# A hybrid decoder layer on one core: who issues the first loads, where the key memsets and the first products of zeros stand

## The chip, the cores and the metric

The kernel runs on one core of a Trainium2 chip. The metric is the device time of one execution in microseconds (us). A core has TensorE (PE: matrix products, with its weight loads in a queue of their own, PEld), VectorE (DVE), ScalarE (ACT), GpSimd (POOL) and SyncE (SP). SP, ScalarE and GpSimd can issue DMA transfers; sixteen DMA engines carry them.

## What is computed

One layer of a decoder for 1024 tokens of width 1024, ahead of which 16 learned meta tokens are put. Everything is in 32-bit floating point.

```python
h = jnp.concatenate([meta, x], axis=1)
u = rmsnorm(h, g_pre_mix[l])
z = u @ w_in[l]
q, k, v, xr, yr = jnp.split(z, split_at, axis=-1)
attn = sliding_window_attention_with_sinks(q, k, v, attn_sinks[l])   # window 128, 8 heads, 2 key heads
...
mix = jnp.concatenate([attn, rec], axis=-1) @ w_out[l]
h = h + rmsnorm(mix, g_post_mix[l])
u = rmsnorm(h, g_pre_ffn[l])
f = jnp.square(jax.nn.relu(u @ w_ff1[l])) @ w_ff2[l]
h = h + rmsnorm(f, g_post_ffn[l])
```

`rec` is a convolution of four steps, a gated linear recurrence over the 1040 tokens and a GeLU gate. The call to the attention is shortened; its heads are reshaped there.

## The kernel before

The kernel is one function, `hybrid_layer`, that lists instructions on tiles. A planner then orders each engine's instructions: it replays the list on a clock of its own, takes what is ready by its place in the list, assigns each tile a buffer of its group (a `slot` of a tag, or a `bank` of the accumulator memory) and adds the waits. Two helpers tie the order by hand where it matters: `behind(name, ins)` puts an instruction behind another one of the same engine, and `chained(e, ins)` (line 332) does so along a list, e = 0 for ScalarE and e = 1 for VectorE.

Every 32-bit operand of a product is split into a high and a low part, and a product is three: high by high, high by low, low by high. ScalarE makes the high part by a cast, VectorE the low part by a subtraction.

The start goes like this, with the lines of the profile. GpSimd makes the identity matrix for the transposes, clears two halves of the key tiles (L298), and makes small constants. SP issues the loads in the order of the list: the meta tokens (L142), two 128-row tiles of x (L147), the two norm weight vectors (L155, L156), the key and value columns of w_in and the first query columns (L384), then further tiles of x. ScalarE loads the table of its square root with a first root of one column (L82).

The norm of the 16 meta rows is `norm_rows`: a square with a sum on ScalarE (L254), the power -1/2 on GpSimd (L170, L176), a scale on VectorE (L260). The first two tiles of x go through `norm_first`. For the first tile the square is shared, half on ScalarE (L237) and half on VectorE (L242); for the second ScalarE squares the whole tile. Then come a root on ScalarE (L82), a reciprocal on VectorE (L199) and two scales of 128x512 (L248).

TensorE meanwhile multiplies zeros: twelve products of 512 columns and six of 256 (`load`, L309), which are never read. Then it transposes the normed rows in eight blocks of 128 columns (`transposed(0, xn)`, L358), each of three pieces (16 meta rows, two tiles of x), and the planner puts one product of zeros of 128 columns beside each block (L365). The banks of the blocks go round over the tags pt, o and s, two banks each. Of each block ScalarE takes the high half, scaled by the norm weight of the column (L117), and VectorE the low half (L118); the norm weights stand in `gcol`, one column per block, which TensorE turns (L160) and VectorE copies (L161). Among the first casts, ahead of blocks 0 and 1, stand two halves of the cast of the key weights (`key_casts`, L344).

With that the first 272 columns of the normed input, u, are there, and TensorE starts with their products for keys and values (`part`, L282): high weights by high u for the eight blocks, high weights by low u, then the same for the values, and the low weights. Queries follow, the next 256 tokens are transposed, and so on for four stages (`ALL`). The stages b = 1, 2, 3 norm their rows by `norm_rows` (in `normed`), two tiles each.

The tile `km` holds the first keys with zeros before them; GpSimd clears it (L412, L413) where the list stands behind the query weights. `vmt` holds the norm weights as rows first; GpSimd clears it later (L589) for other use.

From there on the kernel is products: attention with filling projections, the recurrence, the output projection, and the two large products of the feed-forward part, some of whose blocks are summed first.

Of the kernel before, what the change touches and what calls it, by code (L numbers as in the profile page):

```python
# [10 lines left out]
F32R = mybir.dt.float32r  # L11
AF = mybir.ActivationFunctionType
ALU = mybir.AluOpType
# [3 lines left out]
P = 128  # L17
# [3 lines left out]
NMETA = 16  # L21
# [16 lines left out]
def hybrid_layer(  # L38
# [6 lines left out]
    nc = tc.nc  # L45
# [12 lines left out]
    def slot(tag, shape, dt=F32):  # L58
        uid[0] += 1
        return slab.tile(shape, dt, tag=tag, name=f"{tag}{uid[0]}", bufs=bufs[tag])  # L60
# [4 lines left out]
    def bank(tag, shape=(P, 512)):  # L65
        uid[0] += 1
        return ps.tile(list(shape), F32, tag=tag, name=f"ps_{tag}{uid[0]}")

    def f32(ap):
        return ap.bitcast(F32)  # L70
# [8 lines left out]
    last_lut = [None]  # L79
# [58 lines left out]
    ident = const.tile([P, P], F32, name="ident")  # L138
    make_identity(nc, ident)

    meta_t = slot("d", [NMETA, D])
    nc.sync.dma_start(meta_t, meta_tokens)  # L142
    xt = []

    def load_x(i):
# [6 lines left out]

    vmt = const.tile([P, P], F32, name="vmt")
    g_r = vmt[0:16, :]
    nc.sync.dma_start(g_r[0:8, :], g_pre_mix.rearrange("o (k p) -> (o k) p", p=P))  # L155
    nc.sync.dma_start(g_r[8:16, :], g_pre_ffn.rearrange("o (k p) -> (o k) p", p=P))  # L156

    gcol = const.tile([P, 16], F32, name="gcol")
    pg = bank("o")
    nc.tensor.transpose(pg[:, :16], g_r, ident[:16, :16])  # L160
    nc.vector.tensor_copy(gcol, pg[:, :16])  # L161
    g_mix_col, g_ffn_col = gcol[:, 0:8], gcol[:, 8:16]

    half_pow = const.tile([P, 1], F32, name="half_pow")
# [19 lines left out]
    eps_col = const.tile([P, 1], F32, name="eps_col")  # L184
# [7 lines left out]

    load_root()

    def root_rstd(ssq, bias, n=P):
        sd = small.tile([P, 1], F32, name="sd", tag="sd")
        lut(sd[:n], ssq, AF.Sqrt, bias=bias)
        rs = small.tile([P, 1], F32, name="rs", tag="rs")
        nc.vector.reciprocal(rs[:n], sd[:n])  # L199
        return rs[:n]  # L200


# [29 lines left out]
    def norm_first(src, halves):  # L232

        xn = slot("d", [P, D])
        ss = [small.tile([P, 1], F32, name=f"hq{i}", tag=f"hq{i}") for i in range(2)]
        c = slice(0, 512 if halves else D)
        nc.scalar.activation(  # L237
            xn[:, c], src[:, c], AF.Square, scale=RMS_SC, accum_out=ss[0]
        )
        if halves:  # L240
            c = slice(512, D)
            nc.vector.tensor_tensor_reduce(  # L242
                out=xn[:, c], in0=src[:, c], in1=src[:, c], scale=RMS_SC * RMS_SC,
                scalar=EPS, op0=ALU.mult, op1=ALU.add, accum_out=ss[1],
            )
        rs = root_rstd(ss[0], ss[1] if halves else eps_col)
        for c in (slice(0, 512), slice(512, D)):
            nc.vector.tensor_scalar(xn[:, c], src[:, c], rs, None, op0=ALU.mult)  # L248
        return xn

    def norm_rows(src, n, link=False):
        xn = slot("d", [P, D])
# [46 lines left out]

    zeros = slot("ws", [P, 512], F32R)  # L300
    nc.vector.memset(f32(zeros), 0.0)

    flip = [0]

# [2 lines left out]
    def load(n, cols, after=None):  # L307
        for _ in range(n):
            ins = nc.tensor.matmul(  # L309
                idle[:, :cols], zeros[:, :P], zeros[:, :cols], start=True, stop=True,  # L310
                skip_group_check=True,
            ).ins
            if after:
                behind(after, ins)
        return ins.name

    load(12, 512)
    load(6, 256)

    def normed(b):  # L320
        if b == 0:
            return [
                (norm_rows(meta_t[:NMETA], NMETA), NMETA),
                (norm_first(xt[0], True), P), (norm_first(xt[1], False), P),
            ]
        rows = [(xt[2 * b], P), (xt[2 * b + 1], P)]
        return [(norm_rows(s[:m], m), m) for s, m in rows]


    last = [None, None]  # L330
# [20 lines left out]
    def transposed(b, xn, after=None):  # L351
        t0, n = ALL[b]
        for kc in range(KC):
            flip[0] += 1
            pt = bank(("pt", "o", "s")[flip[0] % 3])
            o = 0
            for s, m in xn:
                ins = nc.tensor.transpose(  # L358
                    pt[:, o : o + m], s[:m, kc * P : (kc + 1) * P], ident[:m, :m]
                )  # L360
                if after:
                    behind(after, ins.ins)
                o += m
            if b == 0:
                load(1, P, ins.ins.name)  # L365
            uh, ul = u[kc]
            if b == 0 and kc in (0, 1):
                key_casts.pop(0)()
            high = split_scaled(
                uh[:, t0 : t0 + n], ul[:, t0 : t0 + n], pt[:, :n],  # L370
                g_mix_col[:, kc : kc + 1],
            )
            if b == 0:
                chained(0, high[0])
                chained(1, high[1])
# [17 lines left out]
    xn = normed(0)  # L393
# [14 lines left out]
    low_w(wv, rv)  # L408
    wq = high_w(rq)
    low_w(wq, rq)  # L410
    km = slot("ws", [P, 4, 2 * P], F32R)
    nc.gpsimd.memset(f32(km[:, 0:2, 0 : P - NMETA]), 0.0)  # L412
    nc.gpsimd.memset(f32(km[:, 2:4, :]), 0.0)  # L413
    nsink = const.tile([P, 8], F32, name="nsink")
    nc.sync.dma_start(nsink, attn_sinks[0].partition_broadcast(P))
    prm_r = slot("d", [8, 512])
# [1211 lines left out]
```

## Time and profile before

| what | us |
|---|---|
| median of 3 runs | 948.82 (948.57 to 948.83) |
| the profiled execution | 949.06 |
| its span, first to last instruction | 947.4 |
| PE busy in the span | 936.9 |
| DVE, ACT, POOL busy | 664.3, 504.3, 133.9 |

The mean granted clock of TensorE in the span was 0.999. All rows of the profile come from the one profiled execution; starts are counted from the first instruction, and its own time stands beside the span because some time lies around it. A row of the timeline gives start, length, engine, line, operation, written tile <- read tiles and, in brackets, how long the engine idled ahead of it and what released it. A row of the chain of waits gives start and length of one piece of the chain that ended last. "SPq" is a DMA being issued by SP. "issue" is time in which the engine waited for nothing that the profile shows. Matmuls are pipelined, so rows of TensorE overlap.

### The profile page before, as it was taken

The numbers are of one execution on the slowest core, as the hardware profiler recorded it, in microseconds if no ns is written. First come the engines' busy times: TensorE is split into PE (matmuls) and PEld (weight loads), VectorE is DVE, ScalarE is ACT, GpSimd is POOL, SyncE is SP. The second block draws the span as 40 slices with busy tenths as digits, with TensorE's granted clock in tenths as the row PEclk, the third lists the DMA queues.
The fourth block names the chain that finished last, engine by engine and source line by source line (L and its number), as shares of the span: only waits on it lengthen the run. The fifth ranks groups of instructions, "written<-read, shape, count | busy, mean of one in ns | idle before, by whom it ended". The sixth has DMA issues, their size and how long they took to land.

```text
span 947.4 us, 12177 instructions
## 1 busy us (share of the span) xinstructions
PE 936.9 (99%) x4584; PEld 783.6 (83%) x4584; DVE 664.3 (70%) x848; ACT 504.3 (53%) x845; POOL 133.9 (14%) x205
## 2 busy tenths in 40 slices
PE   9999999999999999999999999999999999999996
PEld 8999999877788878888888888888888888888885
DVE  6667788889877987665544465476667676779883
ACT  8546765679434664443655575654533443445441
POOL 4104436430021200010000000001111000001201
PEclk9999999999999999999999999999999999999999
DMA  8220011104359659574422364334877756637924
GB/s 273 57 66 25 24 46 45 45 23 140 102 176 271 200 182 285 187 256 134 156 89 89 111 214 121 108 112 112 199 168 176 211 178 194 186 131 209 239 63 89
DMA packets 97366, 134.91 MB, mean 142 GB/s; under 512 B 22230, under 2 KB 61158, under 8 KB 97308
## 3 DMA queue, kind: packets, MB, share of 16 engines
q1 hardware_dynamic: 87996, 108.64, 36.2%
q0 software_dynamic: 8880, 24.19, 12.2%
q10 hardware_dynamic: 432, 1.31, 0.4%
q8 instruction: 36, 0.59, 0.3%
q14 instruction: 22, 0.18, 0.1%
HBM read 112.55 MB, written 20.97 MB: 141 GB/s over the span
## 4 chain that ended last, share of the span: by engine, by line
PE 94%; DVE 3%; issue 1%; DMA 1%; ACT 0%; DVEq 0%; SPq 0%
PE ps_acc L125 11%; PE ps_acc L131 11%; PE ps_acc L130 11%; PE ps_pt L131 6%; PE ps_pt L130 6%; PE ps_pt L125 6%; PE ps_s L125 6%; PE ps_s L131 6%; PE ps_s L130 6%; PE ps_o L125 5%; PE ps_o L130 5%; PE ps_o L131 5%; PE ps_o L699 2%; PE ps_acc L917 1%; PE ps_acc L282 1%
## 5 line engine op out<-in xcount | busy, mean ns | idle before, releaser
L99 DVE TENSOR_TENSOR ws<-raw,ws 128x1024 fp32r<-128x1024 f32 (+1 forms) x69 | 83.1, 1204 | 69.9 <-PE ps_o L130 23.0
L96 ACT CAST ws<-raw 128x1024 fp32r<-128x1024 f32 (+1 forms) x68 | 69.8, 1027 | 82.3 <-PE ps_o L130 33.1
L96 ACT CAST ws<-e 128x1024 fp32r<-128x1024 f32 x41 | 43.0, 1049 | 85.5 <-PE ps_o L130 38.3
L99 DVE TENSOR_TENSOR b<-b,b 128x1024 fp32r<-128x1024 f32 (+1 forms) x49 | 57.5, 1176 | 27.8 <-PE ps_o L130 22.5
L130 PE MATMUL ps_acc<-a,ws 128*128 128x512 f32 (+3 forms) x224 | 76.3, 341 | 0.0
L125 PE MATMUL ps_acc<-a,ws 128*128 128x512 f32 (+3 forms) x224 | 76.3, 341 | 0.0
L131 PE MATMUL ps_acc<-a,ws 128*128 128x512 f32 (+3 forms) x224 | 75.7, 338 | 0.0
L99 DVE TENSOR_TENSOR ws<-e,ws 128x1024 fp32r<-128x1024 f32 x41 | 50.1, 1222 | 31.8 <-ACT ws L96 18.5
L96 ACT CAST b<-b 128x1024 fp32r<-128x1024 f32 (+1 forms) x49 | 49.5, 1011 | 41.7 <-DVE b L1096 35.6
L686 POOL TENSOR_SCALAR_AFFINE_SELECT c<-c 128x512 fp32r<-128x512 f32 x64 | 53.2, 846 | 73.6 <-ACT c L96 64.6
L131 PE MATMUL ps_acc<-ws,b 128*128 128x512 f32 (+1 forms) x120 | 46.1, 384 | 0.0
L130 PE MATMUL ps_acc<-ws,b 128*128 128x512 f32 (+1 forms) x120 | 46.1, 384 | 0.0
L125 PE MATMUL ps_acc<-ws,b 128*128 128x512 f32 (+1 forms) x120 | 46.0, 385 | 0.0
L125 PEld LDWEIGHTS ps_acc<-a,ws 128*128 128x128 f32 x224 | 42.2, 188 | 3.1 <-DVE b L926 0.3
L131 PEld LDWEIGHTS ps_acc<-a,ws 128*128 128x128 f32 x224 | 42.2, 188 | 3.0
L130 PEld LDWEIGHTS ps_acc<-a,ws 128*128 128x128 f32 x224 | 42.1, 188 | 2.8
L125 PE MATMUL ps_pt<-ws,b 128*128 128x512 f32 x112 | 44.3, 395 | 0.0
L130 PE MATMUL ps_pt<-ws,b 128*128 128x512 f32 x112 | 44.2, 395 | 0.0
L131 PE MATMUL ps_pt<-ws,b 128*128 128x512 f32 x112 | 44.0, 392 | 0.0
L125 PE MATMUL ps_s<-ws,b 128*128 128x512 f32 x110 | 43.4, 395 | 0.0
L130 PE MATMUL ps_s<-ws,b 128*128 128x512 f32 x110 | 43.3, 393 | 0.0
L131 PE MATMUL ps_s<-ws,b 128*128 128x512 f32 x110 | 43.2, 393 | 0.0
(421 smaller groups left out, 2682.3 us busy)
## 6 DMA issues: line engine op xcount, KB each, us to landing
raw<-in_w_ff_dram SPq DMA_DIRECT2D x59, 512.0 KB, 3.8
e<-in_w_ff_dram SPq DMA_DIRECT2D x43, 512.0 KB, 3.5
a<-in_w_ff_dram SPq DMA_DIRECT2D x12, 512.0 KB, 6.2
s_dram<-a POOLq DMA_DIRECT2D x12, 512.0 KB, 3.8
raw<-in_w_in_dram SPq DMA_DIRECT2D x9, 512.0 KB, 3.7
c<-in_x_dram SPq DMA_DIRECT2D x8, 512.0 KB, 5.1
d<-in_x_dram SPq DMA_DIRECT2D x8, 512.0 KB, 3.4
out_dram<-raw SPq DMA_DIRECT2D x8, 512.0 KB
```

Source lines behind the costliest of these rows:

```text
L96: cast[0] = nc.scalar.copy(hi, src).ins.name
L99: low = nc.vector.tensor_tensor(lo, src, f32(hi), op=ALU.subtract).ins
L125: ins = nc.tensor.matmul(dst, lh, rh, start=start, stop=False, skip_group_check=True).ins
L130: nc.tensor.matmul(dst, lh, rl, start=False, stop=False, skip_group_check=True)
L131: last_mm[0] = nc.tensor.matmul(dst, ll, rh, start=False, stop=stop, skip_group_check=True).ins.name
L282: last_mm[0] = nc.tensor.matmul(acc[:, :n], w[k // 2][:, kc, :], u[kc][k % 2][:, t0 : t0 + n], start=k == 0 and kc == 0, stop=k == last an ...
L686: nc.gpsimd.affine_select(out=p_[:, :, s], in_=f32(p_[:, :, 0]), pattern=[[0, 4], [g, P]], compare_op=op, fill=0.0, base=0, channel_multip ...
L699: nc.tensor.matmul(two[:, :, oc : oc + w], v, p_.rearrange("p (j i) s c -> p j (i s c)", j=2)[:, :, pc : pc + w], start=n == 0 and k == 0, ...
L917: ins = nc.tensor.matmul(y2_bank[half], (wh, wh, wl)[k][:, kc, :], (uh, ul, uh)[k][:, t0 : t0 + n], start=m % 24 == 0, stop=m % 24 == 23, ...
```

## The change

The meta tokens and the two norm weight vectors are issued by ScalarE's queue; SP's queue begins with the two tiles of x. The transpose of the norm weights stands among the first products of zeros, behind eight of 512 columns; behind it come four of 512 and four of 256. The copy of the turned weights stands between VectorE's half-square of the first tile of x and that tile's reciprocal. The eight products of zeros beside the first transposes are gone. The tile `km` is allocated and cleared at the front, behind the zeros. The second key cast stands ahead of block 2. The order is tied at four more places: the second tile's square behind the first tile's root, its reciprocal behind the first tile's last scale, and the squares and scales of stage b = 2 along the two lists.

```diff
-    nc.sync.dma_start(meta_t, meta_tokens)
+    nc.scalar.dma_start(meta_t, meta_tokens)
...
-    nc.sync.dma_start(g_r[0:8, :], g_pre_mix.rearrange("o (k p) -> (o k) p", p=P))
-    nc.sync.dma_start(g_r[8:16, :], g_pre_ffn.rearrange("o (k p) -> (o k) p", p=P))
+    nc.scalar.dma_start(g_r[0:8, :], g_pre_mix.rearrange("o (k p) -> (o k) p", p=P))
+    nc.scalar.dma_start(g_r[8:16, :], g_pre_ffn.rearrange("o (k p) -> (o k) p", p=P))
 
     gcol = const.tile([P, 16], F32, name="gcol")
-    pg = bank("o")
-    nc.tensor.transpose(pg[:, :16], g_r, ident[:16, :16])
-    nc.vector.tensor_copy(gcol, pg[:, :16])
...
-    def root_rstd(ssq, bias, n=P):
+    def root_rstd(ssq, bias, n=P, after=None):
...
-        nc.vector.reciprocal(rs[:n], sd[:n])
+        ins = nc.vector.reciprocal(rs[:n], sd[:n]).ins
+        if after:
+            behind(after, ins)
...
-        nc.scalar.activation(
+        square = nc.scalar.activation(
             xn[:, c], src[:, c], AF.Square, scale=RMS_SC, accum_out=ss[0]
-        )
+        ).ins
+        if not halves:
+            behind(last_lut[0], square)
...
+            nc.vector.tensor_copy(gcol, pg[:, :16])
-        rs = root_rstd(ss[0], ss[1] if halves else eps_col)
+        rs = root_rstd(ss[0], ss[1] if halves else eps_col, after=scaled[0])
         for c in (slice(0, 512), slice(512, D)):
-            nc.vector.tensor_scalar(xn[:, c], src[:, c], rs, None, op0=ALU.mult)
+            scaled[0] = nc.vector.tensor_scalar(
+                xn[:, c], src[:, c], rs, None, op0=ALU.mult
+            ).ins.name
...
     zeros = slot("ws", [P, 512], F32R)
     nc.vector.memset(f32(zeros), 0.0)
+    km = slot("ws", [P, 4, 2 * P], F32R)
+    nc.gpsimd.memset(f32(km[:, 0:2, 0 : P - NMETA]), 0.0)
+    nc.gpsimd.memset(f32(km[:, 2:4, :]), 0.0)
...
-    load(12, 512)
-    load(6, 256)
+    pg = bank("o")
+    turned = nc.tensor.transpose(pg[:, :16], g_r, ident[:16, :16]).ins
+    behind(load(8, 512), turned)
+    load(4, 512, turned.name)
+    load(4, 256)
...
-        return [(norm_rows(s[:m], m), m) for s, m in rows]
+        return [(norm_rows(s[:m], m, b == 2), m) for s, m in rows]
...
-            if b == 0:
-                load(1, P, ins.ins.name)
             uh, ul = u[kc]
-            if b == 0 and kc in (0, 1):
+            if b == 0 and kc in (0, 2):
                 key_casts.pop(0)()
...
-    km = slot("ws", [P, 4, 2 * P], F32R)
-    nc.gpsimd.memset(f32(km[:, 0:2, 0 : P - NMETA]), 0.0)
-    nc.gpsimd.memset(f32(km[:, 2:4, :]), 0.0)
```

More of the change, by code (lines that the diff above doesn't have):

```diff
@@ L245, in norm_first @@
             )
-        rs = root_rstd(ss[0], ss[1] if halves else eps_col)
+            nc.vector.tensor_copy(gcol, pg[:, :16])
+        rs = root_rstd(ss[0], ss[1] if halves else eps_col, after=scaled[0])
         for c in (slice(0, 512), slice(512, D)):
-            nc.vector.tensor_scalar(xn[:, c], src[:, c], rs, None, op0=ALU.mult)
+            scaled[0] = nc.vector.tensor_scalar(
+                xn[:, c], src[:, c], rs, None, op0=ALU.mult
+            ).ins.name
         return xn
+    scaled = [None]
     def norm_rows(src, n, link=False):
```

## The prediction

> **What bounds the kernel now.** I read the page first: the engines' shares, then the chain that ended last.
>
> ```profile
> span 947.4 us, 12177 instructions
> ...
> PE 936.9 (99%) x4584; PEld 783.6 (83%) x4584; DVE 664.3 (70%) x848; ACT 504.3 (53%) x845; POOL 133.9 (14%) x205
> ...
> PE 94%; DVE 3%; issue 1%; DMA 1%; ACT 0%; DVEq 0%; SPq 0%
> ```
>
> TensorE sets the end nearly everywhere: 94% of the chain is its work. The change takes no instruction out of that 94% except a few products of zeros and otherwise rearranges the first 13 us, before TensorE has enough to do. So what it can move is the moment from which TensorE runs without a gap; all later work follows at that distance. The chain of waits of the first 20 us names that moment:
>
> ```profile
> 0.80 0.40 SPq L142
> 1.26 0.40 SPq L147
> 1.71 4.89 DMA c<-in_x_dram
> 6.62 1.16 ACT d L237 x2
> 7.80 0.30 ACT sd L82
> 8.13 0.17 DVE rs L199
> 8.33 0.79 DVE d L248
> 9.12 0.14 issue
> 9.26 0.30 PE ps_o L358
> ...
> 12.73 5.03 PE ps_acc L282 x37
> ```
>
> The reader is to see one serial path. SP issues the meta tokens, then two tiles of x; the second tile is issued at 1.71 and landed at 6.60 (1.71 + 4.89). ScalarE squares it, takes the root, VectorE inverts and scales, TensorE transposes at 9.26. From 9.26 to 12.73 the chain stays on TensorE in short pieces, but the timeline shows who leads there:
>
> ```profile
> 9.68 0.49 ACT L117 ACTIVATE a<-ps_o,gcol 128x272 fp32r<-128x272 f32 x1 [1.07 <-DVE gcol L161]
> ...
> 12.80 0.53 ACT L117 ACTIVATE a<-ps_s,gcol 128x272 fp32r<-128x272 f32 x1
> ...
> 13.39 4.15 PEld L282 LDWEIGHTS ps_acc<-a,b 128*128 128x128 f32 x33 [0.19 <-ACT a L117]
> ```
>
> ScalarE casts the eight high halves of the transposed input one behind the other, with one key cast among them, from 9.68 to 13.33 (12.80 + 0.53), 3.65 us without a pause. TensorE waits last at 13.39, for the eighth of them; the 33 weight loads from there to 17.54 follow every 0.126 us. So the term to forecast is how much earlier the cast that now starts at 9.68 starts. The 3.65 us behind it keep their nine instructions: the second key cast moves one place later, behind the second cast, and the sum is the same.
>
> **x first on SP's queue.** The meta issue ahead of x costs 0.46 us of SP (0.80 to 1.26). Without it both tiles of x are issued 0.46 us earlier; this is the upper bound of what the second landing gains. The lower bound is a transfer limit. Rows:
>
> ```profile
> 2.00:3.00 1.00, 1.00 (x4) 0.71 (x4) 0.00 (x0) 0.36 (x3) 0.92 (x3) 1.00 0.70 156
> ...
> 5.29 0.63 ACT L237 ACTIVATE d<-c 128x512 f32<-128x512 f32 x1 [1.22 <-DMA c<-in_x_dram]
> ```
>
> The first tile released ScalarE at 5.29, the second, by the chain above, at 6.62: 512 KB in 1.33 us. The meta tokens' 64 KB are an eighth, 0.17 us at that rate. Issued by ScalarE at the same moment, they use the same time as x's start; if nothing of this is hidden, 0.46 - 0.17 = 0.29 us remain. In the third microsecond the DMA engines were busy 0.70 of the time (the stage table's last two columns are DMA share and GB/s), so part of the 64 KB fits in the holes. I take 0.40, and keep 0.29 and 0.46. On this the Trainium skill ("DMA: Bandwidth & Descriptors", section on issuing engines not being separate DMA queues) speaks against hoping for more: another issuing engine saves only the time to issue, since all share the same DMA engines. By it, 0.46 would be the ceiling, as above.
>
> **What ScalarE's three issues push back.** Its nearest issue, and the front of the four engines:
>
> ```profile
> L985 ACTq DMA_DIRECT2D e<-in_g_post_mix_dram x1: 382/382/382, 171.5 to 171.5; - x1
> ```
>
> ```profile
> 0.80 1.28 ACT L82 ACT_TABLE_LOAD   x1 [0.80 <-PEq L1612]
> ...
> 2.18 0.37 SPq L155 DMA_DIRECT2D vmt<-in_g_pre_mix_dram  x1
> ...
> 2.60 0.28 SPq L156 DMA_DIRECT2D vmt<-in_g_pre_ffn_dram  x1
> ...
> 2.92 1.06 ACT L254 ACTIVATE d<-d 16x1024 f32<-16x1024 f32 x1 [0.63 <-DMA d<-in_meta_tokens_dram]
> ...
> 4.16 0.23 POOL L170 TENSOR_SCALAR ms<-ssq 16x1 f32<-16x1 f32 x1 [0.63 <-ACT d L254]
> ...
> 4.73 0.57 POOL L176 TENSOR_TENSOR rs<-ms,half_pow 16x1 f32<-16x1 f32 x1
> ...
> 5.91 0.74 DVE L260 TENSOR_SCALAR d<-d,rs 16x1024 f32<-16x1024 f32 x1
> 6.57 0.14 DVE L199 RECIPROCAL rs<-sd 128x1 f32<-128x1 f32 x1
> ...
> 6.75 0.88 DVE L248 TENSOR_SCALAR d<-c,rs 128x512 f32<-128x512 f32 x2
> ```
>
> Three issues of 0.40, 0.37 and 0.28 us (SP's durations; ScalarE's own row says 0.38 for one) with some 0.05 between are 1.2 us in ScalarE's order ahead of the table load. The table load then ends near 3.3, the small root after it near 3.5, and the meta square starts about 3.5 instead of 2.92: it had 0.63 us of waiting to give up, so it is some 0.6 late, not 1.2. Behind it POOL's root ends at about 5.9 instead of 5.30. VectorE scaled the meta rows at 5.91 only because the half-square of x (L242) came before; now that is done 0.4 earlier, and the meta scale again starts near 5.9. So the first x tile's scaling ends at 7.6 as before (6.75 + 0.88), while the second tile's reciprocal becomes ready at 8.13 - 0.40 = 7.73. Cover: about 0.1 us. What exceeds it is lost one for one, up to the 0.40 gained. SP drops the two weight-vector issues as well and so starts w_in's loads 1.2 us earlier; they stand behind x in the same queue, and no ScalarE cast of them waits in the rows above, so I cost that at nothing.
>
> **The key memsets.** They now run on POOL just when VectorE scales the second x tile:
>
> ```profile
> 8.09 0.28 POOL L412 MEMSET ws<- 128x224 f32 x1
> ...
> 8.31 0.53 POOL L413 MEMSET ws<- 128x512 f32 x1
> ```
>
> ```profile
> L248 DVE TENSOR_SCALAR d<-c,rs x4: 468/482/783, 6.8 to 9.0; 128x512 f32<-128x512 f32 x4
> ```
>
> The four pieces of one size took 0.468 at least, 0.482 in the middle and 0.783 once (minimum, median, maximum), and that once is the piece at 8.33 (0.79 in the chain above), beside the memsets of 8.09 to 8.84. Take them away and 0.783 - 0.468 = 0.31 us go, straight from the chain (the first transpose waits for this piece). Bounds: nothing, if the memsets are not the cause, and 0.31. The row in which both overlap is the nearest there is, so I take 0.31. At the front their 0.81 us cost nothing: POOL waited 0.63 us before 4.16, and that work itself now comes 0.6 later.
>
> **The norm weights and the products of zeros.**
>
> ```profile
> 9.43 0.16 DVE L161 COPY gcol<-ps_o 128x16 f32<-128x16 f32 x1
> ```
>
> ```profile
> 1.51 5.95 PE L309 MATMUL ps_acc<-ws 128*128 128x512 f32 x18 [1.51 <-DVE base_e L563]
> ```
>
> The first cast waited for the copy of the weights, done at 9.59, but the transpose that it reads ended at 9.56 (9.26 + 0.30): 0.03 us to gain. The copy now stands on VectorE between the half-square and the meta scale; queued behind it are that scale, the first x scale and all that follows. It waits for TensorE's transpose of the weights, which stands behind eight of the products of zeros in the row above; at their mean of 0.33 us (5.95 / 18) these end near 4.2. The weights, issued last near 1.7 and landing like the meta tokens 2.1 us on (0.80 to 2.92), come near 3.8. Later than that, TensorE and VectorE wait, but the remaining zeros have nothing behind them before 7.4, and VectorE no input before x. The eight 128-column products among the transposes go, and two of six 256-column ones ahead of them. TensorE waits for ScalarE at 13.39 as it is, and ScalarE has no pause between its casts in which it could have waited for TensorE: I count nothing.
>
> **The link of the third stage's squares** ties them, with their scalings, behind the last weight cast of the first stage, which now comes after the square at 19.15:
>
> ```profile
> 19.15 1.07 ACT L254 ACTIVATE d<-c 128x1024 f32<-128x1024 f32 x1
> ...
> 25.56 0.77 ACT L477 ACTIVATE b<-ps_acc 64x256 fp32r<-64x256 f32 x2 [1.21 <-PE ps_acc L282]
> ```
>
> ScalarE idles 1.21 us before 25.56, and the rows that this square serves are needed only two stages on: no cost. Without that cover up to 1.07 us of the second stage's casts come later.
>
> **Sum.** 0.40 + 0.31 + 0.03 = 0.74 us off the start of TensorE's unbroken run, and the same off the end if nothing behind it takes it back. The profiled execution took 949.06 (947.4 of span and 1.7 around it): 948.32. The median of the plain runs, 948.82, lies 0.24 under the profiled one, so I forecast 948.1, with bounds of 0.29 + 0 + 0 less the lost cover (about 0 in all) and 0.46 + 0.31 + 0.03 = 0.80; with the plain runs' spread (948.57 to 948.83), 947.8 to 948.5 is the forecast's own range, for anything over 0.3 us kept.
>
> **Rivals.** First, the cover is gone: ScalarE's issues or the table load take longer, or x lands no earlier because the transfers are full. Then 0 to 0.3 us remain: 948.5 to 948.8. For it: the 0.1 us of cover; against: 0.63 us of waiting that ScalarE gives up. Chance 0.11.
>
> Second, slower: TensorE's clock is halved at the start.
>
> ```profile
> 938.10:941.60 3.50, 1.63 (x14) 1.00 0.92 132
> 941.60:945.00 3.40, 0.00 (x0) 1.00 0.97 245
> 945.00:947.40 2.40, 0.00 (x0) 0.50 0.15 58
> ```
>
> At the kernel's end (PE busy, clock, DMA share, GB/s) a stretch of 3.4 us with no TensorE work kept the full clock and the next had 0.50; one with 1.63 us of work did not lead to it. After the change the zeros end near 7.1 (7.46 less two), and up to 12.65, where the unbroken run would begin, there are only transposes and, from the first cast's end at 9.43 (9.68 - 0.74 + 0.49), a few real products. If a stretch as thin as 7.1 to 10.5 counts as idle, the clock is half from 10.5 to 13.9: (13.9 - 12.65) / 2 = 0.6 us lost, and 1.7 more if a second stretch follows. The first leaves 948.7, both 948.1 + 2.3 = 950.4, slower than before; the sign turns where half clock lasts past 14.1, (14.1 - 12.65) / 2 = 0.73. Against it: the gap without any product, 7.1 to 9.43, is 2.3 us, shorter than 3.4. Chance 0.05. The Trainium skill ("TensorE: Matmul & The Clock Gate", Parts 1 and 4) says that an idle window of about 3.4 us returns the clock to half, and that transposes do not count as busy. The first half agrees with the 3.4 us row above; no row of before shows the second, and by it this rival would be the one to fear.
>
> Third, the order is sorted anew. The program's order on each engine comes from a planner that replays the kernel on its own clock, and every time at the front moves. It matters where TensorE waits for VectorE:
>
> ```profile
> by line: DVE c L873 26.7%; issue 25.4%; DVE a L99 9.5%; DVE c L871 8.7%; DVE b L872 8.5%; DVE d L757 4.8%; DVE c L872 4.7%; PE ps_pt L131 3.4%; DVE b L99 2.7%; DVE b L878 2.1%; PE ps_pt L125 1.7%; PE ps_pt L130 1.7%; PE ps_o L125 0.8%; PE p
> ```
>
> ```profile
> L99 DVE TENSOR_TENSOR ws<-raw,ws 128x1024 fp32r<-128x1024 f32 (+1 forms) x69 | 83.1, 1204 | 69.9 <-PE ps_o L130 23.0
> ```
>
> The first row is the chain between 222 and 250: VectorE's pieces and the issue between them, hardly TensorE. A piece put ahead there delays one for one: one or two like the subtractions of L99 (1.20 us in the mean, second row) give 948.1 + 1.2 to 2.4 = 949.3 to 950.5, more with a wait behind; put behind, 945.7 to 946.9. Against both: most of the front is tied by hand. Chance 0.12 each way.
>
> **How the numbers follow.** The forecast, 947.8 to 948.5, has 0.60; the cover gone 0.11; the clock 0.05; sorted anew for worse 0.12, for better 0.12. A measurement of this kernel tells about 0.2% from no change: below 946.92 or above 950.72. The forecast, the first rival and most of the clock's lie within. Of the third rival I put 0.08 of the better side beyond, and 0.07 of the worse, with 0.01 of the clock: faster 0.08, same 0.84, slower 0.08. The range of 947.3 to 949.5 takes the forecast, the first rival, the short halved clock and a part of the third rival's, some 0.8 in all.
>
> **What would show it.** The second x tile landing near 6.2; its scale pieces both near 0.47; the first high cast near 8.95 and the eighth's end near 12.6, with TensorE unbroken from there, 0.7 us earlier than 13.39. Wrong would be: a meta scale that ends past 6.7 on VectorE, a granted clock under 1.00 before 17, TensorE's products of the first stage following at 0.23 us instead of 0.126, or a chain between 222 and 250 with other pieces in it than now.

## The result and the profile after

The changed kernel takes 951.21 us (950.60 to 952.14, 10 runs) against 948.67 (948.43 to 949.17, 10 runs) for the kernel before, run beside it: a ratio of 1.0025, 95% interval 1.0017 to 1.0032. It is slower by about a quarter of a per cent. The forecast was 948.1, and the range ended at 949.5.

The page of the changed kernel shows the same work in a longer span; the profiled execution took 951.70 us.

```profile
span 949.9 us, 12157 instructions
...
PE 937.0 (99%) x4574; PEld 782.3 (82%) x4574; DVE 663.8 (70%) x848; ACT 504.3 (53%) x845; POOL 134.8 (14%) x205
```

TensorE is busy for 937.0 us, 0.1 more than before, while the span is 2.5 longer: time went into waits, not into work. Where they are is read from the place at which TensorE's equal pieces stand. First the head, from the timeline of the changed kernel (its line numbers: L319 the products of zeros, L328 the transpose of the norm weights, L371 the transposes of the rows, L267 and L250 the scales, L117 and L118 the high and low halves).

```profile
1.51 3.78 PE L319 MATMUL ps_acc<-ws 128*128 128x512 f32 x8 [1.51 <-DVE base_e L571]
6.12 0.20 PE L328 MATMUL ps_o<-ident,vmt 16*128 16x16 f32 x1 [0.82 <-DMA vmt<-in_g_pre_ffn_dram]
6.25 1.66 PE L319 MATMUL ps_acc<-ws 128*128 128x512 f32 x8
7.84 0.23 PE L371 MATMUL ps_o<-ident,d 16*128 16x16 f32 x1
...
6.06 1.06 ACT L236 ACTIVATE d<-c 128x1024 f32<-128x1024 f32 x1 [0.17 <-DMA c<-in_x_dram]
9.33 0.49 ACT L117 ACTIVATE a<-ps_o,gcol 128x272 fp32r<-128x272 f32 x1 [1.28 <-PE ps_o L371]
...
6.26 0.87 DVE L267 TENSOR_SCALAR d<-d,rs 16x1024 f32<-16x1024 f32 x1 [0.77 <-POOL rs L173]
...
8.22 0.88 DVE L250 TENSOR_SCALAR d<-c,rs 128x512 f32<-128x512 f32 x2
...
13.03 4.16 PEld L289 LDWEIGHTS ps_acc<-a,b 128*128 128x128 f32 x33 [0.19 <-ACT a L117]
```

The unbroken run of 33 weight loads starts at 13.03 instead of 13.39. So the head did gain, but 0.36 us, not 0.74. The second x tile is squared at 6.06 instead of 6.62, and both its scales take 0.88 together instead of 1.17. But the first cast waited 1.28 us for a transpose: TensorE had stopped for the norm weights until 6.12, made the other eight products of zeros behind them, and came to the transposes of the rows at 7.84.

Then the loss. These are the rows of the changed kernel between 20 and 30 us.

```profile
24.97 1.20 PE L289 MATMUL ps_acc<-a,ws 128*128 128x256 f32 x8 [0.78 <-DVE ws L362]
28.14 0.44 PE L371 MATMUL ps_pt<-ident,d 128*128 128x128 f32 x2 [1.63 <-DVE a L118]
29.70 0.27 PE L371 MATMUL ps_s<-ident,d 128*128 128x128 f32 x1
...
23.59 0.17 DVE L553 TENSOR_SCALAR nsink<-nsink 128x8 f32<-128x8 f32 x1 [2.08 <-DMA nsink<-in_attn_sinks_dram]
23.70 1.22 DVE L362 TENSOR_TENSOR ws<-e,ws 128x1024 fp32r<-128x1024 f32 x1
26.82 0.75 DVE L267 TENSOR_SCALAR d<-c,rs 128x1024 f32<-128x1024 f32 x1 [1.01 <-POOL rs L173]
27.60 0.48 DVE L118 SCALAR_TENSOR_TENSOR a<-ps_pt,gcol,a 128x256 fp32r<-128x256 f32 x1
...
23.82 2.00 POOL L627 COPY c<-nsink 128x2 f32<-128x2 f32 x8 [2.83 <-DVE nsink L553]
25.91 0.22 POOL L167 TENSOR_SCALAR ms<-ssq 128x1 f32<-128x1 f32 x1
```

And the same work in the kernel before.

```profile
27.20 0.27 PE L358 MATMUL ps_s<-ident,d 128*128 128x128 f32 x1
...
21.93 1.23 DVE L349 TENSOR_TENSOR ws<-e,ws 128x1024 fp32r<-128x1024 f32 x1
...
24.74 0.48 DVE L118 SCALAR_TENSOR_TENSOR a<-ps_pt,gcol,a 128x256 fp32r<-128x256 f32 x1
25.14 0.16 DVE L545 TENSOR_SCALAR nsink<-nsink 128x8 f32<-128x8 f32 x1
...
21.24 0.22 POOL L170 TENSOR_SCALAR ms<-ssq 128x1 f32<-128x1 f32 x1
25.37 1.04 POOL L619 COPY c<-nsink 128x2 f32<-128x2 f32 x8 [3.10 <-DVE nsink L545]
```

The reader is to see one exchange on VectorE. The negation of the attention sinks (`nsink`), eight columns and 0.17 us of work, waits for a load that lands at 23.56. Before, it stood behind the first low half of stage b = 1, at 25.14, and found the load landed. Now it stands ahead of the low part of the second query weights (L362, before L349), and VectorE, which takes its instructions in order, stands still for 2.08 us. That low part starts at 23.70 instead of 21.93. GpSimd has the same exchange: the eight copies of the negated sinks stand ahead of the root of the fifth x tile, which runs at 25.91 instead of 21.24; VectorE waits again at 26.82, and the first low half comes at 27.60 instead of 24.74. TensorE waits 0.78 and 1.63 us for the two. A transpose that stood at 27.20 stands at 29.70: with the 0.36 that the head had gained, 2.86 are lost there. The chain of waits of the changed kernel goes the same way, from the load to the scale of the fifth tile:

```profile
16.28 7.28 DMA nsink<-in_attn_sinks_dram
...
23.82 2.00 POOL c L627 x8
...
25.91 0.23 POOL ms L167
...
26.82 0.75 DVE d L267
```

### The profile page after: what moved, and what is told of

The parts are those of the page before. It is cut to its first block, busy times and chain, and to the rows that moved or that the text cites. A ratio compares the mean times of both kernels' runs of the same rounds, so it can differ in the third digit from the quotient of the medians.

```text
span 949.9 us, 12157 instructions
## 1 busy us (share of the span) xinstructions
PE 937.0 (99%) x4574; PEld 782.3 (82%) x4574; DVE 663.8 (70%) x848; ACT 504.3 (53%) x845; POOL 134.8 (14%) x205
## 4 chain that ended last, share of the span: by engine, by line
PE 92%; DVE 3%; SPq 1%; DMA 1%; issue 1%; POOL 0%; DVEq 0%
PE ps_acc L125 11%; PE ps_acc L131 11%; PE ps_acc L130 11%; PE ps_pt L131 6%; PE ps_pt L130 6%; PE ps_pt L125 6%; PE ps_s L131 6%; PE ps_s L125 6%; PE ps_s L130 6%; PE ps_o L125 5%; PE ps_o L130 5%; PE ps_o L131 5%; PE ps_o L707 2%; PE ps_acc L925 1%; PE ps_s L637 1%
```

## The experiments

Theory: the planner, whose clock moved with the front, put the negation of the sinks ahead of work that TensorE waits for. First rival: the link of the squares of stage b = 2, which moved the fifth tile's square, root and scale. Second rival: TensorE's clock at the start. After the first four runs theory A held the order and the clock together as two causes; the letters in the later expectations go by that. All kernels were timed beside the kernel before, in three groups of four; it took 948.87 us (948.23 to 950.25), 948.86 (948.24 to 950.34) and 948.60 (948.05 to 950.09).

| run | median, us | runs, us | ratio to before (95% interval) |
|---|---|---|---|
| e1 sinks late | 950.57 | 948.77 to 949.35 (5), 950.57 to 952.06 (6) | 1.0010 (1.0000 to 1.0019) |
| e2 no link | 951.02 | 949.66 to 950.40 (5), 951.02, 951.95 to 952.46 (5) | 1.0021 (1.0012 to 1.0029) |
| e3 sinks late, zeros first | 949.12 | 948.84 to 950.17 | 1.0001 (0.9992 to 1.0010) |
| e4 memsets at the front alone | 948.54 | 948.24 to 949.09 | 0.9995 (0.9986 to 1.0003) |
| e5 sinks late, no hole | 948.82 | 948.48 to 949.41 | 1.0000 (0.9991 to 1.0009) |
| e6 sinks early, no hole | 949.83 | 949.37 to 951.15 | 1.0011 (1.0002 to 1.0020) |
| e7 before, thin | 948.58 | 948.18 to 949.25 (10), 950.39 | 0.9998 (0.9989 to 1.0007) |
| e8 sinks late, hole | 950.48 | 948.66 to 948.96 (4), 950.21 to 951.47 (7) | 1.0013 (1.0004 to 1.0022) |
| e9 x first, sinks late | 949.07 | 948.62 to 949.28 | 1.0003 (0.9994 to 1.0012) |
| e10 x first, sinks late, hole | 951.63 | 949.66 to 950.01 (3), 951.42 to 952.79 (5) | 1.0029 (1.0019 to 1.0039) |
| e11 before, thin, sinks late | 948.75 | 948.45 to 949.39 (10), 951.02 | 1.0002 (0.9994 to 1.0011) |
| e12 e11 with memsets at the front | 948.50 | 948.22 to 948.94 (10), 950.43 | 0.9999 (0.9990 to 1.0008) |

### e1: the negation tied late

On the changed kernel, with `low_b1` the first low half of stage b = 1:

```diff
-    nc.vector.tensor_scalar(nsink, nsink, -1.0, None, op0=ALU.mult)
+    behind(low_b1[0], nc.vector.tensor_scalar(
+        nsink, nsink, -1.0, None, op0=ALU.mult
+    ).ins)
```

> The changed kernel with one more tie: the negation of the sinks stands behind the first low half of stage b = 1 on VectorE, where it stood before the change. Theory (order): the changed kernel loses at two waits of TensorE at 24.97 (0.78 us, for the low part of the second query weights) and 28.14 (1.63 us, for the first low half of stage 1), because the planner put the negation, which waits for a load that lands at 23.5, ahead of that low part, and the copies of the negated sinks ahead of the root of the fifth x tile on GpSimd. With the tie both go: 948.3 (947.9 to 948.8), VectorE without the 2.1 us wait. Rival (front): the loss comes from the first 13 us, where the weights land late and in some runs the clock is halved: 950.8 to 951.4. Rival (link): the loss comes from the fifth tile's square standing later: 951 as well, with VectorE waiting for GpSimd's root near 23.

The times fell into two heaps. Five of eleven runs came back to the kernel before; six stayed near 951. So the order is one cause and there is another, which comes and goes from run to run. The profiled execution was one of the long ones, and its head shows why:

```profile
1.51 3.78 PE L319 MATMUL ps_acc<-ws 128*128 128x512 f32 x8 [1.51 <-DVE base_e L577]
6.29 0.26 PE L328 MATMUL ps_o<-ident,vmt 16*128 16x16 f32 x1 [1.00 <-POOL rs L173]
6.48 2.93 PE L319 MATMUL ps_acc<-ws 128*128 128x512 f32 x8
9.34 0.28 PE L373 MATMUL ps_o<-ident,d 16*128 16x16 f32 x1
```

The eight products of zeros behind the transpose of the norm weights (four of 512, four of 256 columns) took 2.93 us; in the profile of the changed kernel they took 1.66. TensorE ran at half clock, and the trace's first record of the full clock stands at 14.50 us; in the profile of the changed kernel it stands at 5.50. The transposes of the rows therefore begin at 9.34 instead of 7.84, and TensorE's products stand 2.2 us later than before up to 28 us. (The column named PEclk prints 1.00 before the first record of a trace; here the length of equal products tells the clock.)

### e2: without the link

```diff
-        return [(norm_rows(s[:m], m, b == 2), m) for s, m in rows]
+        return [(norm_rows(s[:m], m), m) for s, m in rows]
```

> The changed kernel without the link of stage b = 2. The negation still stands ahead of the second query weights' low part, but the fifth tile's root stands ahead of the sinks' copies on GpSimd. Order theory: the first wait stays (VectorE idle until 23.6, TensorE 0.8 us near 25), the second goes or shrinks: 949.0 to 949.8. Rival (link alone): back to 948.3. Rival (front): 951.2.

The times fell into two heaps here too, and the median, 951.02, lies between them; so it tells little beside the 951.21 of the changed kernel. The link is not the whole cause: even the lower heap is 0.8 to 1.5 us above the 948.87 of the kernel before. But the lower heap ends at 950.40, and no run of the changed kernel is below 950.60. That has the direction that the order theory expected of this run, a smaller second wait, though it gave 949.0 to 949.8: without the link the fifth tile's root stands ahead of the sinks' copies (at 22.27 in the profiled execution). The profiled execution is of the upper heap, with the full clock only from 14.51, so the waits of the lower heap are not shown, and the share of the link stays open.

### e3: the negation late, and no hole among the zeros

Beside e1's edit:

```diff
-    behind(load(8, 512), turned)
-    load(4, 512, turned.name)
-    load(4, 256)
+    behind(load(12, 512), turned)
+    load(4, 256, turned.name)
```

> As e1, and the transpose of the norm weights behind all twelve products of 512 columns, with only the four of 256 behind it. The weights landed at 6.1 in the changed kernel, TensorE waited 0.82 us for them and the transposes of the rows began at 7.84 instead of 7.40, so the first cast started at 9.33 instead of the forecast 8.95. Here the twelve products run to about 6.6 and hide the landing: first cast at 8.95 to 9.0, 0.35 us less than e1: 947.9 to 948.1. If the late landing is not what holds the first cast, the same as e1.

949.12, and no run above 950.17: the upper heap is gone with TensorE's stop among the zeros. In the profiled execution, the longest of the eleven, the clock was full from 6.09 and then halved once more, as the windows of that run show (TensorE's busy time, then those of the other engines; the third figure from the end is the granted clock):

```profile
9.50:12.90 3.40, 3.37 (x16) 1.91 (x14) 2.86 (x7) 3.40 (x10) 0.00 (x0) 1.00 1.06 311
12.90:16.30 3.40, 3.40 (x15) 3.40 (x16) 3.40 (x5) 3.40 (x5) 0.47 (x1) 0.50 0.98 233
```

This is the thin stretch that the prediction's second rival named. TensorE looks busy in 9.50 to 12.90, 3.37 of 3.40 us, but with 16 matrix instructions, transposes among them, and the next stretch had half the clock. That a transpose does not count as busy the way a product does is what the Trainium skill says ("TensorE: Matmul & The Clock Gate", Part 4); this run agrees. In e7's profiled execution, with the same products missing, no stretch was halved.

### e4: the key memsets alone

On the kernel before, `km` allocated and cleared behind `zeros`, as in the change.

> The kernel before with the key memsets at the front and nothing else. If they slow VectorE's scale at 8.33 by the 0.31 us of the forecast, that scale takes 0.47 and the time falls to 948.35 (0.3 less). If they do not, 948.67 and the scale still takes 0.78.

948.54. The profiled execution has its first high cast at 8.94 and its unbroken run at 12.64, the 0.74 of the forecast, although nothing was done to x: the second tile's square started at 6.16 there, and its scales took 0.88 together. At the end of that execution nothing is left of it. 0.38 went near 27.5 us, where TensorE waited 0.22 for a low half of the queries. What lies behind that is a load again: ScalarE waited 0.64 us for the fifth tile of x, the cast of the second query weights came behind its square, and VectorE waited 0.41 us at 21.57 for that cast.

```profile
19.02 1.07 ACT L254 ACTIVATE d<-c 128x1024 f32<-128x1024 f32 x1 [0.64 <-DMA c<-in_x_dram]
```

Another 0.5 went between 320 and 400 us; why there was not tried.

### e5: both suspects out

e3 and, beside it, the eight 128-column products of zeros back among the first transposes (`if b == 0: load(1, P, ins.ins.name)`).

> The changed kernel with both suspects out: the sinks' negation tied behind the first low half of stage b=1, all twelve 512-column products of zeros ahead of the transpose of the norm weights (so that TensorE has no hole while it waits for them), and the eight 128-column products of zeros back among the first transposes. Theory A (order of VectorE and GpSimd around the sinks' load, plus TensorE's clock at the start): the clock is at 1.00 from about 6 us on in every run, TensorE's products follow at least 0.35 us earlier than before from 13.5 us on, and the time is 948.0 to 948.6, no run above 949.5. Rival B (order alone, clock of no account): the median is that of the run with the negation tied late and nothing else, 950.6, or what its quick runs took, 948.8 to 949.3, with the same two heaps of times. Rival C (the head itself, x first with the other loads on ScalarE, costs time): 949.5 to 951 although neither wait nor halved clock is seen.

948.82 in one heap, the time of the kernel before. The loss of the changed kernel is gone, and with it rival C. The time is 0.2 above the upper end of what theory A gave. In its profile the head itself gained hardly anything: the full clock came only at 7.17, the transposes begin at 7.83 (7.40 before) and the first cast at 9.57 (9.68 before).

### e6: the order alone

e5's front, with the negation in its place of the changed kernel, ahead of the second query weights' low part, by `chained(1, ...)`.

> The same front as the run without hole, but the sinks' negation ahead of the low part of the second query weights, as in the changed kernel; on GpSimd four of the eight sink copies stand between the two steps of the fifth x tile's root. Theory A: the clock is at 1.00 from about 6 us on, and the two waits of TensorE near 25 and 28 us are there by themselves: 2.0 to 3.1 us over the run without hole, 950.2 to 951.4 with one heap of times. Rival B' (the clock at the start makes all of the loss, the waits are absorbed): within 0.4 us of the run without hole, 948.0 to 949.0.

949.83 in one heap but for one run, 1.0 more than e5. The negation waited 1.17 us and TensorE 0.72 behind it:

```profile
22.42 0.17 DVE L525 TENSOR_SCALAR nsink<-nsink 128x8 f32<-128x8 f32 x1 [1.17 <-DMA nsink<-in_attn_sinks_dram]
...
26.09 0.44 PE L370 MATMUL ps_pt<-ident,d 128*128 128x128 f32 x2 [0.72 <-DVE a L118]
```

Less than expected, for two reasons in the rows: the load landed at 22.4 here, not 23.56, and only four of the eight copies stand ahead of the fifth tile's root. So the order costs by itself, and its price hangs on how late the load lands.

### e7: the thin stretch alone

On the kernel before:

```diff
-            if b == 0:
-                load(1, P, ins.ins.name)
```

> The kernel before without the eight products of zeros among its first transposes, nothing else. Theory A (a stretch with hardly more than transposes can halve TensorE's clock): some runs as before, some 1 to 2 us longer, median 948.9 to 950.5, and in a run of the longer kind a granted clock of 0.5 between about 10 and 17 us. Rival B: as before within 0.3 us, since these products are read by nobody and TensorE waits for ScalarE beside them; then the removal costs nothing by itself.

948.58, ten of eleven runs at or below 949.25. The zero products among the transposes can be taken out at no cost that shows. The one run of 950.39 is no sign of a halved clock by itself: ten of the 96 runs of the kernel before, which has these products, took 949.81 to 950.34. What those long runs are is not shown. The profiled execution shows how a gain at the head is taken back, with the order as it was:

```profile
24.89 0.17 DVE L543 TENSOR_SCALAR nsink<-nsink 128x8 f32<-128x8 f32 x1 [0.40 <-DMA nsink<-in_attn_sinks_dram]
...
27.65 0.36 PE L125 MATMUL ps_acc<-a,b 128*128 128x256 f32 x1 [0.33 <-DVE b L478]
```

Its unbroken run starts at 12.65, 0.74 earlier. The sinks' load does not land earlier (24.86, against 23.61 in the kernel before), so the negation waits 0.40 and TensorE 0.33.

### e8: the hole alone, in the changed kernel

e1's edit and the eight 128-column products of zeros among the transposes; the hole ahead of the norm weights' transpose stays.

> The changed kernel with the negation tied late and the eight 128-column products of zeros back among the first transposes, but the hole of TensorE ahead of the transpose of the norm weights left as it is. Theory A says that the hole delays the release of the clock: two heaps of times remain, one near 948.3 (released near 5.5), one 1.0 to 2.2 us above it (released at 11 to 14.5). Rival D (only the thin stretch of transposes matters): one heap near 948.3.

Two heaps again, four runs near 948.7 and seven near 951; against e5, which differs in the hole alone, the median is 1.66 higher. The profiled execution is one of the lower heap:

```profile
1.51 3.51 PE L319 MATMUL ps_acc<-ws 128*128 128x512 f32 x8 [1.51 <-DVE base_e L579]
6.18 0.20 PE L328 MATMUL ps_o<-ident,vmt 16*128 16x16 f32 x1 [1.16 <-POOL rs L173]
6.32 1.67 PE L319 MATMUL ps_acc<-ws 128*128 128x512 f32 x8
```

Its hole is as long as e1's, but the full clock came at 4.58, ahead of the hole: the eight products ahead of it took 3.51 instead of 3.78, those behind it 1.67 instead of 2.93. Rival D falls: with all zero products back the upper heap is still there.

### e9 and e10: x first in the kernel before, without and with the hole

e9 is the kernel before with the three loads issued by ScalarE and the negation tied behind the sixth low half of stage b = 1. e10 is e9 with the transpose of the norm weights behind eight of its products of zeros.

> The kernel before with the loads of the meta tokens and norm weights issued by ScalarE, and the sinks' negation tied behind the sixth low half of stage b=1 so that its wait reaches nobody. Prediction's step (x issued 0.46 earlier lands 0.40 earlier than 6.60): the second x tile's square near 6.2 and TensorE's products from 13.5 us on 0.4 earlier than in the profile of before. Rival: that profile had a late landing by chance, since kernels with the old issue order squared the second tile at 6.16; then x first is worth 0.1 us or less, and the table load that starts at 2.16 instead of 0.80 eats it: 948.6 to 949.0.

> The same as the x-first run with late negation, and beside it only the transpose of the norm weights moved behind eight of the products of zeros, so that TensorE has a hole there. Theory A: the hole alone splits the times into two heaps, one near the x-first run's, one 1.0 to 2.5 us above it, although the zero products among the transposes are all there. Rival D (the hole costs only its own length, hidden as the zeros have nothing behind them): same as the x-first run within 0.3 us.

e10 against e9: 951.63 against 949.07, three runs near 949.9 and five from 951.4 on. The hole by itself makes the second heap in the old kernel too. e10's profiled execution is of the upper one: its ten zero products behind the hole took 3.35 us, and the full clock came at 14.48.

e9 shows what x first brings and why it does not arrive:

```profile
6.00 1.06 ACT L237 ACTIVATE d<-c 128x1024 f32<-128x1024 f32 x1 [0.56 <-DMA c<-in_x_dram]
7.06 0.28 ACT L82 ACTIVATE sd<-hq,hq 128x1 f32<-128x1 f32 x1
9.94 0.49 ACT L117 ACTIVATE a<-ps_o,gcol 128x272 fp32r<-128x272 f32 x1 [1.79 <-PE ps_pt L360]
...
6.19 0.74 DVE L260 TENSOR_SCALAR d<-d,rs 16x1024 f32<-16x1024 f32 x1 [0.77 <-POOL rs L176]
7.63 2.13 DVE L248 TENSOR_SCALAR d<-c,rs 128x512 f32<-128x512 f32 x4
...
8.69 0.80 POOL L417 MEMSET ws<- 128x512 f32 x1
```

The second tile is squared at 6.00. But the planner puts the first tile's root behind that square, at 7.06, so that all four scales come after it, and the key memsets run beside them: 2.13 us for the four. In e10 the memsets are over before 7.8, and the same four take 1.66:

```profile
7.57 1.66 DVE L245 TENSOR_SCALAR d<-c,rs 128x512 f32<-128x512 f32 x4
...
7.18 0.53 POOL L418 MEMSET ws<- 128x512 f32 x1
```

### e11 and e12: what the experiments point to

e11 is e7 with the negation behind the sixth low half of stage b = 1; e12 is e11 with the key memsets at the front.

> The kernel before without the eight products of zeros among its first transposes, and the sinks' negation behind the sixth low half of stage b=1. In the run without these products TensorE came 0.73 earlier at 13.5 us and kept only 0.26 behind 28 us, as VectorE waited 0.40 us for the sinks' load and TensorE 0.33 us behind that. If the load is what takes the gain back, 0.6 to 0.75 remain to the end: 948.1 to 948.3. If something else in that stage does, 948.5 as without the tie.

> As the run before it, and the key memsets at the front as well: all that the experiments point to, on the kernel before. TensorE's unbroken run 0.75 to 1.0 earlier than in the profile of before, kept to the end: 947.9 to 948.3 if the clock is released near 6 us in each run; a heap 1 to 2 us above where it is not. If the memsets' place is of no account by itself, the same as the run before it.

948.75 and 948.50 against 948.60 for the kernel before: no gain that can be told. In e11's profiled execution the second tile's square started at 7.25, so its head says nothing of the tie, and the question of that run stays open. In e12's, TensorE came 0.43 earlier at 13.5 us, the negation waited for nothing, and by 28 us TensorE was 0.18 late: the wait had moved to the cast of the second query weights, for which VectorE waited 0.66 at 22.11. As in e4, ScalarE had waited ahead of that cast, for the load of the fifth x tile:

```profile
19.56 1.07 ACT L254 ACTIVATE d<-c 128x1024 f32<-128x1024 f32 x1 [0.85 <-DMA c<-in_x_dram]
```

No version here beats the kernel before by a difference that can be told.

## Why the prediction was wrong, point by point

**What fails first: "the remaining zeros have nothing behind them before 7.4".** The prediction let the norm weights land near 3.8, by the meta tokens' 2.1 us. They were issued at 1.85 and landed about 6.1, although they are 4 KB each and on another queue than x's two tiles, which were under way at the same time. A late landing was weighed and priced at nothing, and that was wrong twice. The eight zeros ahead of the stop also ended at 5.29 (1.51 + 3.78), not near 4.2: the mean of 0.33 us by which they were priced mixed products of 512 and of 256 columns, some of them behind the clock's release at 6.34. The zeros behind the stop ended at 7.84, so TensorE reached the transposes 0.44 later than before, and the first cast came at 9.33 instead of the forecast 8.95. This is most of the 0.38 by which the head's gain fell short. And the zeros are there for the clock: a stop among them can leave TensorE at half clock up to 14.5 us. The second rival gave the halved clock 0.05 and looked for it behind the zeros; it mostly came from a release at the start that was missed. e5 against e8 (1.66) and e9 against e10 (2.56) show the price.

**The third rival was right in kind and wrong in place and size.** "The order is sorted anew" had 0.12 on the worse side, 1.2 to 2.4 us, in the stage from 222 to 250. It came at 23 us, where the prediction had looked at the link alone, and it cost 2.9 in the profiled execution (0.36 earlier became 2.50 late). The term mis-sized was a piece put ahead, priced by its own length; "more with a wait behind" was named there and given no price. The piece is 0.17 us long; what it costs is the landing of what it waits for, 23.56, less the place that it takes, 21.5. The rows of before had it:

```profile
16.15 0.62 SPq L415 DMA_DIRECT2D nsink<-in_attn_sinks_dram  x1
```

The load of the sinks was issued at 16.15 and took 7.5 us to land, so it landed near 23.6; the negation stood at 25.14, only 1.5 us behind that, and the neighbour that it now precedes stood at 21.93, ahead of that landing. That the order did it is shown by e1, which moves nothing else and brings back five runs of eleven, and by e6 against e5.

**Why the two causes do not add up.** e8 loses 1.66 by the hole and e6 1.0 by a part of the order; the changed kernel loses 2.4 against e5. Its profiled execution lost 2.86 at the order, with the full clock already from 5.50. That a late clock hides part of this, since VectorE then comes late to the place where the load is waited for, is argued and not shown. In e2's profiled execution, with the full clock only at 14.51, the negation ran at 25.92 and waited for nothing; but there the load had landed at 21.29, and the negation would not have waited some 2.6 us earlier either. The landing moves: from 21.26 to 25.36 over the fourteen profiles. So the price of the order can differ from run to run by itself, and why the changed kernel has one heap of times where e1 has two stays open.

**x first: right.** The second x tile's square was forecast near 6.2 and started at 6.06. In the nine profiles with the loads on ScalarE it started at 5.83 to 6.32, in the five with the old issue at 6.16 to 7.25 (before: 6.62). The gain of 0.40 is of that size, but the landing moves by as much from one execution to the next, so a term of 0.40 read from one profile was not safe to half its size.

**The cover: wrong.** These are ScalarE's first rows in the changed kernel.

```profile
0.80 0.42 ACTq L142 DMA_DIRECT2D d<-in_meta_tokens_dram  x1
1.25 0.57 ACTq L155 DMA_DIRECT2D vmt<-in_g_pre_mix_dram  x1
1.85 0.28 ACTq L156 DMA_DIRECT2D vmt<-in_g_pre_ffn_dram  x1
2.16 1.28 ACT L82 ACT_TABLE_LOAD   x1 [2.16 <-issue]
...
3.80 1.05 ACT L261 ACTIVATE d<-d 16x1024 f32<-16x1024 f32 x1
```

The issues took 0.42, 0.57 and 0.28 us, the table load began at 2.16 instead of 0.80, and the meta square at 3.80, where 3.5 was forecast. The meta scale was to start near 5.9 and started at 6.26; with 0.87 us it ended past the 6.7 that the prediction gave as the mark of being wrong. Everything on VectorE behind it moved: the second tile's scales started at 8.22, 0.11 earlier than before, where 0.40 had been hoped for. The copy of the turned weights did no harm there: the planner put it behind the meta scale and the reciprocal, at 7.12, so that VectorE did not wait for the late weights.

**The memsets: right.** The two scales took 0.88 us instead of 1.17, 0.29 of the forecast 0.31, with the memsets elsewhere; e9 and e10 show the same price from the other side, 0.47 for four scales.

**The link: "no cost" is not shown, and its reason was too narrow.** The prediction looked at ScalarE's idle time and at when TensorE needs the rows. In the changed kernel the fifth tile's square starts at 20.63 instead of 19.15, its root comes behind the sinks' copies, and its scale stands on VectorE ahead of the first low half of stage b = 1, which TensorE needs at once: the 1.01 us that VectorE waits ahead of 26.82 are for this root. With the negation late the link does no visible harm (e5), so it costs through the order if it costs; e2's lower heap points the same way, and leaves the size open.

**The products of zeros among the transposes: right for the kernel before**, by e7; but e3 shows that with the other edits their absence can halve the clock once.

**What the prediction did not ask.** In these profiles a gain at the head met the next thing that did not move with it: in e7 the load of the sinks, in e4 and e12 the load of the fifth x tile. e7 and e4 had the whole 0.74 at 13.5 us and kept 0.26 and 0.36 at 28. So no version without the two losses brought 0.74, and e5, with both out, took the time before.

## What to carry to other kernels

Where a planner orders the work, list the instructions that stand within a few us of the landing of what they wait for, read that landing from more than one profile (the sinks' moved by 4.1 us here), and price an exchange with a neighbour by the landing less the neighbour's place, not by the length of the piece. Filling products that keep a clock up must not wait for a load; put whatever waits behind them. A gain at the head is worth what is left of it at the first load that does not come earlier: look for that load before summing.

## What the runs showed of the hardware

**The clock's release hangs on the phase.** In the traces the full clock comes at the end of a stretch of 3.4 us whose place differs from run to run. The full clock lasted 938.66 us in the kernel before (6.34 to 945.00) and 931.84 in e1 (14.50 to 946.33), 275 and 273 times 3.413 us, and the halved stretch of e3 was 3.41 us long (12.92 to 16.33). TensorE begins its zeros at 1.51 or 1.52 in every profile. Where no hole follows, the release came between 5.8 and 7.2 us; with the hole it came at 4.58 (e8) and 5.50 (the changed kernel), or not before 14.48 to 14.51 (e1, e2, e10). Of the 30 runs of e1, e8 and e10, 12 lie in the lower heap. An estimate from the rows: in e8 3.07 us of work, from 1.51 to 4.58, were enough for the release, and the zeros end at 5.29, so a stretch may hold some 0.34 us without work; to be counted it must end between 4.58 and 5.63, in 1.05 of 3.4 us or three runs in ten. The Trainium skill ("TensorE: Matmul & The Clock Gate", Part 1) has the window at 3413 ns, free-running, and the clock going up after one busy window; the traces agree, and add that a stop of 0.9 to 1.3 us can be enough to miss it; e8's, of 1.16 us, came after its release. Why in e1 no earlier stretch between 7.7 and 14.5, with transposes and products, brought the release was not tried.

**Small loads landed late beside large ones of another queue.** The 4 KB of norm weights took some 4.3 us from issue to use, the 64 KB of meta tokens, issued 1 us earlier, 2.98. The Trainium skill ("DMA: Bandwidth & Descriptors", on issuing engines not being separate DMA queues) says that transfers of different issuing engines run on the same DMA engines and interleave; these times agree, though no run here moved the large loads away to show it.

**GpSimd's memsets and VectorE's scales slow each other.** Beside four scales of 2.13 us the 128x512 memset took 0.80; apart from them it took 0.53 and the scales 1.66. The Trainium skill ("SBUF — State Buffer", on who interferes with whom) puts this down to a port pair that the two share, taken by one at a time; these rows agree with a cost to both.
